# Decay matrices of a gated DeltaNet kept in DRAM, and beta and decay applied per token at R

## The chip, the cores and the metric

The kernel runs on one core of a Trainium2 chip. The core has TensorE (PE, with its weight loads listed as PEld), VectorE (DVE), ScalarE (ACT), GpSimd (POOL) and SyncE (SP), which issues nearly all DMAs. The metric is the device time of one launch in microseconds, the median of several runs.

## The reference

One inference step of a two-layer decoder on 1104 tokens (1024 prompt tokens behind 16 learned ones, and 8 samples of 8 tokens), width 1024. Layer 0 mixes tokens with a gated DeltaNet of 8 heads of 128, layer 1 with a pooling mixer; a gated ConvFFN (2816 wide) follows each. What matters here is the DeltaNet's chunked recurrence:

```python
G = jnp.cumsum(g, axis=-1)
decay = jnp.exp(jnp.where(causal, G[..., :, None] - G[..., None, :], -jnp.inf))
kk = jnp.einsum('bhnid,bhnjd->bhnij', k, k)
lower = jnp.where(strict, beta[..., :, None] * kk * decay, 0.0)
T = lax.linalg.triangular_solve(lower + eye, ...)          # inverse, per chunk
U = jnp.einsum('bhnij,bhnje->bhnie', T, v * beta[..., None])
W = jnp.einsum('bhnij,bhnjd->bhnid', T, k * (beta * jnp.exp(G))[..., None])
A = jnp.einsum('bhnid,bhnjd->bhnij', q, k) * decay
q_dec = q * jnp.exp(G)[..., None]
k_dec = k * jnp.exp(G[..., -1:] - G)[..., None]
def step(S, blk):
    v_new = U_c - W_c @ S
    o = q_dec_c @ S + A_c @ v_new
    S = S * g_tot_c + k_dec_c.T @ v_new
```

So every chunk of every head needs the decay matrix twice: for the triangular inverse and for A. Behind the recurrence o is normalised, gated by z and multiplied by w_out, and the result is added to the residual x.

## The kernel before

Everything is float32. Large products are three TensorE passes on operands that are split into a high and a low part (mm3, L258 to L266); the recurrence's own products are single float32 matmuls of 128 by 128. Tokens stand in nine blocks of 128 (NU): eight of the prompt, and a last one with 16 prompt tokens and the 64 sample tokens ("tail", NTAIL = 80 tokens). GROUPS is three groups of three blocks.

**Stage A (0 to 520 us).** Input projection, causal conv, l2-norm, and for each head k_steps (L479 to L512): it loads the row G of accumulated log decays and the row of beta, broadcast to all partitions (Gb L484, Bb L485), makes E = G_j - G_i plus a mask on DVE (L490, nine instructions), E = exp(E) on ACT (L493), E = E*beta on POOL (L494), stores k (kd, L497), and multiplies k kT by E into Q on DVE (L504). Triangular inverses follow.

**Stage C, the recurrence (520 to about 835 us).** For head h, chain(h) (L1006) walks the eight prompt blocks in order. A block is: pp = (k*exp(G)*beta) S on PE (L1023), R = bv - pp on DVE (L1025), op = q_dec S on PE (L1026), pv = Q R on PE (L1030), vn = pv on ACT (L1032), pS = kd vn on PE (L1036), the new S on DVE (L1041), op += AT vn on PE (L1043). tail(h) (L1058) does the last block. The chain is a string of dependences, so a function weave (L1203) runs fillers between its steps: nxt(h) (L1165), which prepares head h+1, and wouts (L1127), the product with w_out of earlier pairs of heads.

prep(h) (L896) is, for each group: begin() with exp(G) on ACT (L916) and three subtractions on DVE that make E again (L919); scaled() with exp(E) on ACT (L927) and three POOL products, kq[0] = q*exp(G) (L928), eG = exp(G)*beta (L929), kq[1] = k*eG (L930); qk = k q on PE (L937); AT = qk*E on DVE (L939); six transposes of k and v on PE (L944), which ACT scales into kd and bv (L949). begin, scaled and the rest reach their engines through a list (later_on) that the chain empties step by step, so they stand among the chain's instructions on ACT, DVE and POOL in an order fixed when the program is written out.

load(h) (L710) fetches G, beta, q, k and v of a head from DRAM, 576 KB each, each into a tile with one buffer; it is called as soon as the previous head's prep is written out, and each load waits until the last reader of its tile is done. nxt(0) ends with the three loads of the residual x (xT, L1181, 1472 KB each). SP issues DMAs in program order.

gated (L964) normalises o (osq on ACT and DVE, L975 and L986; osb on DVE, L976) as a side job. early_norm (L1122), at the end of stage C, takes the sum of squares of the residual for the first ConvFFN; its tiles come from CT.tile (L1111), out of the five buffers of kq. Behind stage C the ConvFFNs and the pooling mixer run to 2581 us; their weights come through Stream (SP load L161, cast on ACT L153, low part on POOL L154).

Of the kernel before, what the change touches and what calls it, by code (L numbers as in the profile page):

```python
# [10 lines left out]
F32 = mybir.dt.float32  # L11
# [185 lines left out]
def build(nc, tc, I, O, stop=None):  # L197
# [136 lines left out]
    Qd_d = dr.tile([H, P, NTP], F32, name="Qd")  # L334

# [5 lines left out]
    brow_d = dr.tile([H, NTP], F32, name="brow")  # L341

# [136 lines left out]
    def k_steps(h, kT):  # L479
# [14 lines left out]
        G.tensor_tensor(E, E, Bb, op=ALU.mult)  # L494
        Q = kp.tile([P, NU, P], F32, tag="Q", name="Q", bufs=2)
        yield 7
        SY.dma_start(out=kd_d[h], in_=kT)  # L497
        for g0, gn in GROUPS:
            ps = px.tile([P, 3, P], F32, tag="px", name="kk")
            for u in range(gn):  # L500
                s = slice((g0 + u) * P, (g0 + u + 1) * P)
                T.matmul(ps[:, u, :], kT[:, s], kT[:, s], start=True, stop=True)
            q = Q[:, g0:g0 + gn, :]
            V.tensor_tensor(q, ps, v3(E[:, g0 * P:(g0 + gn) * P]), op=ALU.mult)  # L504
            G.affine_select(q, q, pattern=[[0, gn], [1, P]], compare_op=ALU.not_equal, fill=1.0,
                            base=0, channel_multiplier=-1)
            yield 1
# [199 lines left out]
    cl = None  # L707
    Xbd = Tbd = None

    def load(h):  # L710

        t = heads.setdefault(h, {})
        for nm in "GBkqv":
            t[nm] = cl.tile([P, NTP], F32, tag="l" + nm, name="l" + nm)
        SY.dma_start(out=t["G"], in_=grow_d[h:h + 1, :].partition_broadcast(P))
        SY.dma_start(out=t["B"], in_=brow_d[h:h + 1, :].partition_broadcast(P))
        for nm, src in (("q", qd_d), ("k", kd_d), ("v", vd_d)):
            SY.dma_start(out=t[nm], in_=src[h])
# [177 lines left out]
    def prep(h):  # L896
        t = heads[h]
        Gb, Bb = t["G"], t["B"]
# [6 lines left out]
        for gi, (g0, gn) in enumerate(GROUPS):  # L905
# [6 lines left out]
            E = c1.tile([P, 3, P], F32, tag="E", name="E", bufs=2)  # L912
            eG = c1.tile([P, 3, P], F32, tag="eG", name="eG", bufs=2)

            def begin():
                A.activation(eG, v3(Gb[:, s]), AF.Exp)  # L916
                for u in range(gn):
                    m = cm[:, K_MF:K_MF + P] if g0 + u < 8 else cm[:, K_MT:K_MT + P]
                    V.scalar_tensor_tensor(E[:, u, :], Gb[:, (g0 + u) * P:(g0 + u + 1) * P],  # L919
                                           cols[:, g0 + u, 1, h:h + 1], m, op0=ALU.subtract, op1=ALU.add)  # L920
            later_on(begin)
            yield from pause(0.15)
            kq = c2.tile([P, 2, gn, P], F32, tag="kq", name="kq", bufs=5)
            q2 = tl("q2")

            def scaled():
                A.activation(E, E, AF.Exp)  # L927
                G.tensor_tensor(kq[:, 0], v3(t["q"][:, s]), eG, op=ALU.mult)  # L928
                G.tensor_tensor(eG, eG, v3(Bb[:, s]), op=ALU.mult)  # L929
                G.tensor_tensor(kq[:, 1], v3(t["k"][:, s]), eG, op=ALU.mult)  # L930
                A.activation(q2, v3(t["q"][:, s]), AF.Square, scale=P * EPS ** 0.5)
            later_on(scaled)
# [73 lines left out]
    def chain(h):  # L1006
# [5 lines left out]
        for gi, (g0, gn) in enumerate(GROUPS):  # L1012
# [45 lines left out]
    def tail(h, op):  # L1058
# [3 lines left out]
        kq, kd, bv, AT = (t[nm][6] for nm in ("kq", "kd", "bv", "AT"))  # L1062
# [15 lines left out]
        V.tensor_tensor(R[:n], bv[:n, u, :], pp[:n, :P], op=ALU.subtract)  # L1078
# [26 lines left out]
    class CT:  # L1105
# [93 lines left out]
    for h in range(H):  # L1199
# [3 lines left out]
        weave(chain(h), 24.0, [(cur, 7.9 if h else 10.8, 0.0, 0.88, True), (wo, 11.0 if h > 1 else 6.0, 0.0 if h > 1 else 0.45, 1.0, False)], flush_pend)  # L1203
# [481 lines left out]
```

## Time and profile before

| | us |
|---|---|
| median of 3 runs | 2586.09 |
| lowest, highest | 2578.38, 2588.12 |
| the profiled execution's own time | 2583.61 |
| its span in the profile | 2581.5 |
| mean granted TensorE clock | 0.978 |

The profiled execution is the one that all rows below come from. Its span is the time between the first and the last instruction that the profile shows; some 2 us of its own time lie around that. It is 2.5 us below the median of the runs. A stretch is a window from one time in the span to another; in views by window the columns are the busy microseconds and the number of instructions of each engine, the granted clock of TensorE (PEclk, 1.00 is 2.4 GHz and 0.50 is 1.2 GHz), the busy share of the 16 DMA engines, and GB/s.

### The profile page before, as it was taken

What the parts mean: (1) busy time and instruction counts of PE and PEld (TensorE: products, weight loads), DVE (VectorE), ACT (ScalarE), POOL (GpSimd) and SP (SyncE); (2) the same over time, 40 slices, a digit from 0 to 9 for tenths busy, and PEclk for the clock granted to TensorE, in tenths of its full rate; (3) what the DMA queues carried; (4) which work ended last, traced back from release to release, by engine and by line L of the source; (5) the groups of instructions that cost most, each with busy time, mean ns of one, the idle gap of its engine ahead of it and who ended that gap; (6) DMA issues with size and microseconds to landing.
All of it is one profiled execution on the core that took longest, in us unless ns stands there. A gap on an engine that the chain in (4) does not pass through costs nothing.

```text
span 2581.5 us, 38414 instructions
## 1 busy us (share of the span) xinstructions
PE 2415.2 (94%) x14341; PEld 2355.8 (91%) x14341; DVE 1629.9 (63%) x3156; ACT 1029.1 (40%) x2169; POOL 1056.6 (41%) x1103
## 2 busy tenths in 40 slices
PE   6898989979999799999999999888999999999997
PEld 6898988868888799999999999878899999999996
DVE  7566799655666655555555547897964555555556
ACT  5667322354554533322222344445354323223234
POOL 3455322154553443322332465566465333223342
PEclk9999999988999899999999999999999999999999
DMA  3255422476451111111111132233433111111112
GB/s 133 96 183 170 155 78 79 175 251 193 145 176 58 59 53 54 44 39 50 42 50 41 63 111 94 90 110 106 91 100 102 54 46 44 39 50 46 46 54 81
DMA packets 139930, 235.41 MB, mean 91 GB/s; under 512 B 48976, under 2 KB 59600, under 8 KB 139360
## 3 DMA queue, kind: packets, MB, share of 16 engines
q1 hardware_dynamic: 139744, 232.96, 27.3%
q8 instruction: 113, 1.85, 0.3%
q14 instruction: 73, 0.60, 0.1%
HBM read 191.77 MB, written 41.14 MB: 90 GB/s over the span
## 4 chain that ended last, share of the span: by engine, by line
PE 67%; DVE 20%; ACT 5%; issue 3%; POOL 3%; DMA 2%; SPq 0%; DVEq 0%; POOLq 0%; ACTq 0%
PE up L262 12%; PE up L264 12%; PE up L263 12%; PE dn L264 6%; PE dn L262 6%; PE dn L263 6%; DVE acc L385 3%; DVE tb L523 2%; DVE X L525 2%; POOL wlo L154 2%; DVE nhf L317 1%; PE ps L262 1%; PE ps L263 1%; PE ps L264 1%; DVE acc L1262 1%
## 5 line engine op out<-in xcount | busy, mean ns | idle before, releaser
L154 POOL TENSOR_TENSOR wlo<-wst,whi 128x512 fp32r<-128x512 f32 x470 | 631.7, 1362 | 642.3 <-ACT whi L153 629.3
L262 PE MATMUL up<-hhi,whi 128*128 128x370 f32 (+2 forms) x2112 | 709.0, 336 | 0.7 <-ACT hhi L320 0.7
L263 PE MATMUL up<-hlo,whi 128*128 128x370 f32 (+2 forms) x2112 | 700.1, 331 | 2.7 <-DVE hlo L323 1.8
L264 PE MATMUL up<-hhi,wlo 128*128 128x370 f32 (+2 forms) x2112 | 701.5, 332 | 0.0
L1262 DVE SCALAR_TENSOR_TENSOR acc<-up,cv,acc 128x368 f32<-128x368 f32 (+4 forms) x528 | 303.7, 575 | 625.5 <-ACT acc L1254 388.3
L1326 DVE TENSOR_TENSOR xT<-xT,dn 128x368 f32<-128x368 f32 (+1 forms) x864 | 408.9, 527 | 2.4 <-PE dn L264 2.3
L263 PEld LDWEIGHTS up<-hlo,whi 128*128 128x128 f32 x2112 | 402.0, 190 | 5.9 <-DVE hlo L323 2.2
L262 PEld LDWEIGHTS up<-hhi,whi 128*128 128x128 f32 x2112 | 400.4, 190 | 3.0 <-ACT hhi L320 1.0
L264 PEld LDWEIGHTS up<-hhi,wlo 128*128 128x128 f32 x2112 | 400.2, 189 | 0.0
L262 PE MATMUL dn<-ghi,whi 128*128 128x368 f32 (+1 forms) x1056 | 352.9, 334 | 21.7 <-DVE xT L1326 12.4
L264 PE MATMUL dn<-ghi,wlo 128*128 128x368 f32 (+1 forms) x1056 | 349.2, 331 | 0.5 <-POOL wlo L154 0.5
L263 PE MATMUL dn<-glo,whi 128*128 128x368 f32 (+1 forms) x1056 | 348.9, 330 | 0.3 <-POOL glo L1300 0.3
L1254 ACT ACTIVATE acc<-up,cv 128x368 f32<-128x368 f32 (+1 forms) x264 | 173.0, 655 | 431.0 <-PE up L264 429.1
L1300 POOL TENSOR_TENSOR glo<-acc,ghi 128x368 fp32r<-128x368 f32 (+1 forms) x132 | 133.2, 1009 | 485.8 <-ACT ghi L1299 475.9
L262 PE MATMUL ps<-hhi,whi 128*128 128x368 f32 (+1 forms) x792 | 273.5, 345 | 35.2 <-DVE acc L385 29.6
L153 ACT CAST whi<-wst 128x512 fp32r<-128x512 f32 x470 | 274.6, 615 | 78.2 <-PE up L263 50.0
L263 PE MATMUL ps<-hlo,whi 128*128 128x368 f32 (+1 forms) x792 | 269.6, 340 | 5.2 <-DVE hlo L323 3.8
L264 PE MATMUL ps<-hhi,wlo 128*128 128x368 f32 (+1 forms) x792 | 268.3, 339 | 0.0
L262 PEld LDWEIGHTS dn<-ghi,whi 128*128 128x128 f32 x1056 | 200.6, 190 | 26.0 <-DVE xT L1326 7.7
L263 PEld LDWEIGHTS dn<-glo,whi 128*128 128x128 f32 x1056 | 200.7, 190 | 2.0 <-POOL glo L1300 0.6
L264 PEld LDWEIGHTS dn<-ghi,wlo 128*128 128x128 f32 x1056 | 200.5, 190 | 1.0 <-POOL wlo L154 1.0
L262 PEld LDWEIGHTS ps<-hhi,whi 128*128 128x128 f32 x792 | 154.2, 195 | 42.1 <-issue 29.8
(207 smaller groups left out, 3262.8 us busy)
## 6 DMA issues: line engine op xcount, KB each, us to landing
wst<-i_w_up SPq DMA_DIRECT2D x272, 256.0 KB, 2.8
wst<-i_w_dn SPq DMA_DIRECT2D x120, 256.0 KB, 2.7
wst<-i_w_in SPq DMA_DIRECT2D x62, 256.0 KB, 2.8
Gb<-grow SPq DMA_DIRECT2D x8, 576.0 KB, 4.7
Bb<-brow SPq DMA_DIRECT2D x8, 576.0 KB
vd<-out SPq DMA_DIRECT2D x8, 576.0 KB, 2.8
zd<-out SPq DMA_DIRECT2D x8, 576.0 KB, 5.9
kd<-out SPq DMA_DIRECT2D x8, 576.0 KB, 4.1
```

The lines of the kernel that those rows point to most:

```text
L153: self.nc.scalar.copy(hi, st)
L154: self.nc.gpsimd.tensor_tensor(lo, st, hi.bitcast(F32), op=ALU.subtract)
L262: T.matmul(ps, hi[:, ws], rhi(k), start=start and j == 0, stop=False)
L263: T.matmul(ps, hi[:, ws], rlo(k), start=False, stop=False)
L264: T.matmul(ps, lo[:, ws], rhi(k), start=False, stop=stop and j == n - 1)
L385: V.scalar_tensor_tensor(acc[:, a:n], ps[:, o + a - d:o + n - d], w[3 - d], acc[:, a:n], op0=ALU.mult, op1=ALU.add)
L523: V.tensor_tensor(t, X[:n, 0:k, j:j + 1].to_broadcast([n, k, w]), Qb[:n, j:j + 1, j + 1:m].to_broadcast([n, k, w]), op=ALU.mult)
L525: V.tensor_tensor(X[:n, 0:k, j + 1:m], X[:n, 0:k, j + 1:m], t, op=ALU.subtract)
L1254: A.activation(acc[:, b:], ps[:, o + b:o + CH], AF.Identity, scale=w[2], bias=col(C_FCB + l * NUP + n))
L1262: V.scalar_tensor_tensor(acc[:, i:m], ps[:, o + i - d:o + m - d], w[2 - d], acc[:, i:m], op0=ALU.mult, op1=ALU.add)
L1300: G.tensor_tensor(glo, acc, ghi.bitcast(F32), op=ALU.subtract)
L1326: V.tensor_tensor(xT[:, m, s], xT[:, m, s], ps[:, b:CH], op=ALU.add)
```

## The change

In stage A, the exponentiated decay matrix E of each head is stored to DRAM (Ed, 576 KB a head) before k; the POOL product with beta writes to Q instead of E, and DVE multiplies in Q. In stage C, load(h) fetches E instead of beta (five loads as before), and k goes to one of three buffers in rotation instead of one. prep(h) no longer makes E (begin is gone, exp(G) moves into scaled) and has one POOL product a group instead of three; in the last group a POOL and an ACT copy of 128 by 80 fill a tile qk for the tail. In the chain pp = k S is taken from k unscaled, and R = pp*c + bv, where c = -beta*exp(G) stands per token in cols, made once for all heads ahead of the recurrence. early_norm's tiles come from the load tiles of G, q and v instead of kq. The loads of xT move from the end of nxt(0) to right behind load(1). Two cost figures of weave change. The number of TensorE instructions does not.

```diff
@@ k_steps
         A.activation(E, E, AF.Exp)
-        G.tensor_tensor(E, E, Bb, op=ALU.mult)
         Q = kp.tile([P, NU, P], F32, tag="Q", name="Q", bufs=2)
+        G.tensor_tensor(flat(Q), E, Bb, op=ALU.mult)
         yield 7
+        SY.dma_start(out=Ed_d[h], in_=E)
         SY.dma_start(out=kd_d[h], in_=kT)
...
-            V.tensor_tensor(q, ps, v3(E[:, g0 * P:(g0 + gn) * P]), op=ALU.mult)
+            V.tensor_tensor(q, ps, q, op=ALU.mult)
@@ load
-        for nm in "GBkqv":
+        for nm in "GEqv":
             t[nm] = cl.tile([P, NTP], F32, tag="l" + nm, name="l" + nm)
+        t["k"] = (c1 if h % 3 else cl).tile([P, NTP], F32, tag=f"lk{h % 3}", name="lk")
         SY.dma_start(out=t["G"], in_=grow_d[h:h + 1, :].partition_broadcast(P))
-        SY.dma_start(out=t["B"], in_=brow_d[h:h + 1, :].partition_broadcast(P))
-        for nm, src in (("q", qd_d), ("k", kd_d), ("v", vd_d)):
+        for nm, src in (("q", qd_d), ("k", kd_d), ("E", Ed_d), ("v", vd_d)):
             SY.dma_start(out=t[nm], in_=src[h])
@@ prep
-            E = c1.tile([P, 3, P], F32, tag="E", name="E", bufs=2)
+            E = v3(t["E"][:, s])
-            def begin():
+            kq, q2 = tl("kq"), tl("q2")
+            def scaled():
                 A.activation(eG, v3(Gb[:, s]), AF.Exp)
-                for u in range(gn):
-                    m = cm[:, K_MF:K_MF + P] if g0 + u < 8 else cm[:, K_MT:K_MT + P]
-                    V.scalar_tensor_tensor(E[:, u, :], Gb[:, (g0 + u) * P:(g0 + u + 1) * P],
-                                           cols[:, g0 + u, 1, h:h + 1], m, op0=ALU.subtract, op1=ALU.add)
-            later_on(begin)
-            yield from pause(0.15)
-            kq = c2.tile([P, 2, gn, P], F32, tag="kq", name="kq", bufs=5)
-            q2 = tl("q2")
-            def scaled():
-                A.activation(E, E, AF.Exp)
-                G.tensor_tensor(kq[:, 0], v3(t["q"][:, s]), eG, op=ALU.mult)
-                G.tensor_tensor(eG, eG, v3(Bb[:, s]), op=ALU.mult)
-                G.tensor_tensor(kq[:, 1], v3(t["k"][:, s]), eG, op=ALU.mult)
+                G.tensor_tensor(kq, v3(t["q"][:, s]), eG, op=ALU.mult)
                 A.activation(q2, v3(t["q"][:, s]), AF.Square, scale=P * EPS ** 0.5)
+                if gi == 2:
+                    t["qk"] = c2.tile([P, 2, NTAIL], F32, tag="qk", name="qk")
+                    G.tensor_copy(t["qk"][:, 0, :], kq[:, 2, :NTAIL])
+                    A.copy(t["qk"][:, 1, :], t["k"][:, TAIL0:NT])
@@ chain (tail alike)
-                    T.matmul(pp, kq[:, 1, u, :], S, start=True, stop=True)
+                    T.matmul(pp, t["k"][:, c * P:(c + 1) * P], S, start=True, stop=True)
                     R = c2.tile([P, P], F32, tag="R", name="R")
-                    V.tensor_tensor(R, bv[:, u, :], pp, op=ALU.subtract)
+                    V.scalar_tensor_tensor(R, pp, cols[:, c, 1, h:h + 1], bv[:, u, :], op0=ALU.mult, op1=ALU.add)
@@ behind lnexp()
+    A.activation(cols[:, :, 1, :], cols[:, :, 1, :], AF.Exp)
+    V.scalar_tensor_tensor(cols[:, :, 1, :], cols[:, :, 1, :], -1.0, cols[:, :, 0, :], op0=ALU.mult, op1=ALU.mult)
@@ nxt
             load(1)
+            for c in range(NCH):
+                SY.dma_start(out=xT[:, :, ck_(c)], in_=I["xT"][c])
             wd.fetch()
...
             if h == 0:
-                for c in range(NCH):
-                    SY.dma_start(out=xT[:, :, ck_(c)], in_=I["xT"][c])
                 wd.need(1)
```

The order of the instructions shows it at three places. The first is SP's queue during head 0's chain, before: the loads of head 1 (lG, lB, lq, lk, lv), those of w_out and z, the loads of head 2, then xT.

```order
L715 DMA lG<-grow 128x1152
L716 DMA lB<-brow 128x1152
L718 DMA lq<-qd_83 128x1152
L718 DMA lk<-kd_75 128x1152
L718 DMA lv<-vd_91 128x1152
L161 DMA wst<-i_w_out 128x512 x2
L957 DMA lz<-zd_99 128x384 x2
L715 DMA lG<-grow 128x1152
L716 DMA lB<-brow 128x1152
L718 DMA lq<-qd_84 128x1152
L718 DMA lk<-kd_76 128x1152
```

The same place after (the lines are those of the changed kernel).

```order
L720 DMA lG<-grow 128x1152
L722 DMA lq<-qd_83 128x1152
L722 DMA lk<-kd_75 128x1152
L722 DMA lE<-Ed_108 128x1152
L722 DMA lv<-vd_91 128x1152
L1170 DMA xT<-i_xT 128x8x368 x3
L161 DMA wst<-i_w_out 128x512 x2
L954 DMA lz<-zd_99 128x384 x2
L720 DMA lG<-grow 128x1152
L722 DMA lq<-qd_84 128x1152
L722 DMA lk<-kd_76 128x1152
```

xT has moved ahead of the loads of w_out, z and head 2, behind those of head 1; head 2's k stands third in its set instead of fourth.

The second place is DVE's queue in a head in the middle of the recurrence, before: the new S, the subtractions for E, R, two rows of other work, and AT.

```order
L1041 SCALAR_TENSOR_TENSOR S_4844<-S_4843,eGl,pc_4845 128x128
L919 SCALAR_TENSOR_TENSOR E<-lG,cols,cm 128x128 x3
L1025 TENSOR_TENSOR R<-bv,pc_4845 128x128
L1150 TENSOR_TENSOR xT<-xT,wo 128x384
L975 TENSOR_TENSOR osq<-osq,q_6155 128x384
L976 SCALAR_TENSOR_TENSOR osb<-op,cv,lz 128x384
L939 TENSOR_TENSOR AT<-qk,E 128x384
```

The same queue after.

```order
L1038 SCALAR_TENSOR_TENSOR S_4860<-S_4859,eGl,pc_4861 128x128
L1022 SCALAR_TENSOR_TENSOR R<-pc_4861,cols,bv 128x128
L936 TENSOR_TENSOR AT<-qk,lE 128x384
L1148 TENSOR_TENSOR xT<-xT,wo 128x384
L972 TENSOR_TENSOR osq<-osq,q_6080 128x384
L973 SCALAR_TENSOR_TENSOR osb<-op,cv,lz 128x384
```

Nothing stands between the new S and R now, R has another form, and AT stands ahead of the residual's addition and of osq.

The third place is PE's queue where head 0's chain ends and its tail begins, before: the tail's pp, the last block's pv, pS and op, two steps of the tail, and the first qk of head 2.

```order
L1070 MATMUL pp<-kq,Sall 128x2x8 x8
L1030 MATMUL pc_4845<-bv,lQ 128x128
L1036 MATMUL pc_4845<-vn,kd 128x128
L1043 MATMUL op<-AT,vn 128x128
L1075 MATMUL pp<-cm,kqS 80x128
L1076 MATMUL op<-kqS,cm 128x80
L937 MATMUL qk<-lq,lk 128x128 x3
```

The same place after.

```order
L1067 MATMUL pp<-qk,Sall 128x2x8 x8
L1027 MATMUL pc_4861<-bv,lQ 128x128
L934 MATMUL qk<-lq,lk 128x128 x3
L1033 MATMUL pc_4861<-vn,kd 128x128
L1040 MATMUL op<-AT,vn 128x128
L1072 MATMUL pp<-cm,kqS 80x128
L1073 MATMUL op<-kqS,cm 128x80
```

The first qk of head 2 has moved four instructions ahead.

## Rows read from the trace of the kernel before

**Rows 1.** The page: the span, and the busy time of each engine.

```profile
span 2581.5 us, 38414 instructions
PE 2415.2 (94%) x14341; PEld 2355.8 (91%) x14341; DVE 1629.9 (63%) x3156; ACT 1029.1 (40%) x2169; POOL 1056.6 (41%) x1103
```

**Rows 2.** The view by windows, one window a head: from the tail's first pp of one head to that of the next, heads 2 to 6 of the chain. The first number behind the window is its length; then PE, PEld, DVE, ACT and POOL busy with their counts, PEclk, the DMA share and GB/s.

```profile
603.80:642.89 39.09, 36.55 (x261) 34.83 (x261) 25.38 (x61) 19.11 (x57) 17.25 (x16) 0.96 0.48 142
642.89:680.64 37.75, 34.79 (x262) 32.59 (x261) 25.63 (x60) 21.01 (x61) 22.73 (x20) 1.00 0.51 163
680.64:718.25 37.61, 35.06 (x262) 33.35 (x261) 25.18 (x60) 19.12 (x57) 17.08 (x16) 1.00 0.56 171
718.25:755.07 36.82, 34.23 (x263) 32.42 (x261) 24.96 (x60) 20.66 (x60) 21.08 (x19) 1.00 0.50 161
755.07:792.65 37.58, 35.04 (x262) 33.33 (x261) 25.18 (x60) 19.64 (x58) 18.33 (x17) 1.00 0.34 96
```

**Rows 3.** The waits of PE in the same stretch, 603.8 to 792.65 us: who waits, for what, us in total, times, longest.

```profile
PE tr L944 <- DVE AT L939: 5.0, 5, 1.9
PE pc L1030 <- DVE R L1025: 4.2, 4, 1.1
PE tr L944 <- ACT osq L986: 3.5, 5, 0.7
```

**Rows 4.** The timeline of head 4 at one such wait: start, duration, engine, line; in brackets how long the engine had idled and for what.

```profile
694.00 2.97 DVE L919 SCALAR_TENSOR_TENSOR E<-lG,cols,cm 128x128 f32<-128x128 f32 x3
696.89 0.28 DVE L1025 TENSOR_TENSOR R<-bv,pc 128x128 f32<-128x128 f32 x1
697.00 0.52 ACT L927 ACTIVATE E<-E 128x384 f32<-128x384 f32 x1 [2.55 <-DVE E L919]
697.22 0.49 PE L1030 MATMUL pc<-R,lQ 128*128 128x128 f32 x2 [1.03 <-DVE R L1025]
698.42 0.55 PE L944 MATMUL tr<-cm,lv 128*128 128x128 f32 x3 [0.71 <-ACT osq L986]
```

**Rows 5.** The view by windows in head 7's chain, where no prep is left to run.

```profile
780.00:790.00 10.00, 10.00 (x80) 9.99 (x79) 5.34 (x13) 4.16 (x13) 3.98 (x4) 1.00 0.01 2
```

**Rows 6.** All instructions of one line or tile: the subtractions for E, R, and the form of R after the change (the new S at L1041, the same operation with the same kinds of operands but for the side that PSUM is on): least, mean and greatest ns, first and last start.

```profile
L919 DVE SCALAR_TENSOR_TENSOR E<-lG,cols,cm x72: 335/805/2193, 512.7 to 776.6; 128x128 f32<-128x128 f32 x72
L1025 DVE TENSOR_TENSOR R<-bv,pc x56: 271/286/290, 528.4 to 817.0; 128x128 f32<-128x128 f32 x56
L1041 DVE SCALAR_TENSOR_TENSOR Sall<-S,eGl,pc x8: 346/346/351, 553.4 to 819.5; 128x128 f32<-128x128 f32 x8
```

**Rows 7.** The view by windows at the start of the recurrence, heads 0 and 1, and one short stretch of head 2.

```profile
525.00:542.20 17.20, 15.91 (x108) 14.23 (x108) 9.45 (x23) 10.98 (x35) 8.32 (x9) 0.90 0.95 278
542.20:559.80 17.60, 12.79 (x91) 10.70 (x91) 11.21 (x24) 13.49 (x42) 13.06 (x13) 1.00 0.38 124
559.80:565.40 5.60, 0.00 (x1) 0.03 (x1) 4.00 (x4) 0.94 (x2) 5.00 (x5) 0.55 1.00 373
565.40:580.90 15.50, 12.36 (x78) 11.53 (x78) 9.41 (x24) 6.43 (x21) 5.53 (x6) 0.83 1.06 389
580.90:591.00 10.10, 9.37 (x40) 8.32 (x39) 3.78 (x10) 6.15 (x20) 4.84 (x5) 0.50 0.75 180
621.00:626.00 5.00, 4.42 (x21) 4.42 (x21) 2.50 (x7) 3.47 (x13) 1.00 (x1) 0.66 0.00 0
```

**Rows 8.** The timeline of the same stretch, SP's DMA issues (SPq) and the first qk of head 2 on PE.

```profile
532.62 0.32 SPq L715 DMA_DIRECT2D lG<-grow  x1
554.74 0.32 SPq L715 DMA_DIRECT2D lG<-grow  x1
557.91 0.32 SPq L718 DMA_DIRECT2D lk<-kd  x1
559.19 8.04 SPq L1181 DMA_DIRECT2D xT<-i_xT  x3
565.40 1.62 PE L937 MATMUL qk<-lq,lk 128*128 128x128 f32 x6 [5.62 <-DMA lk<-kd]
```

**Rows 9.** The view by windows where the loads of head 1, then those of head 2, then xT keep the DMA engines full, and where nothing is under way.

```profile
538.00:545.00 7.00, 5.75 (x43) 4.88 (x42) 4.99 (x9) 2.17 (x7) 3.36 (x4) 1.00 0.98 383
546.00:555.00 9.00, 6.79 (x46) 5.49 (x46) 5.20 (x15) 8.00 (x26) 5.43 (x6) 1.00 0.00 2
566.00:581.00 15.00, 11.86 (x77) 10.93 (x76) 9.51 (x24) 6.53 (x21) 4.93 (x6) 0.84 1.06 387
```

**Rows 10.** Stage A: DVE's wait for the broadcast rows Gb in 100 to 300 us, in the view of waits (us in total, times, longest).

```profile
DVE E L490 <- DMA Gb<-grow: 35.7, 6, 7.0
```

**Rows 11.** The view by windows in stage A, two stretches between loads and stores.

```profile
216.00:221.00 5.00, 2.75 (x10) 2.62 (x11) 4.35 (x10) 3.28 (x5) 2.54 (x5) 0.80 0.04 15
236.00:240.00 4.00, 3.51 (x20) 3.37 (x21) 3.38 (x9) 3.94 (x6) 2.62 (x6) 1.00 0.03 5
```

**Rows 12.** The page's DMA issues, the store of k in stage A: KB each, median us from issue to landing.

```profile
kd<-out SPq DMA_DIRECT2D x8, 576.0 KB, 4.1
```

**Rows 13.** The timeline at the end of the recurrence: the first loads of the ConvFFN's weights, early_norm's sum of squares on PE, and the first cast of those weights on ACT.

```profile
829.96 30.21 SPq L161 DMA_DIRECT2D wst<-i_w_up  x8
841.48 0.78 PE L295 MATMUL ss<-nac,ck 128*128 128x368 f32 x2
848.50 1.14 ACT L153 CAST whi<-wst 128x512 fp32r<-128x512 f32 x2
```

More of the change, by code (lines that the diff above doesn't have):

```diff
@@ L334, in build @@
     Qd_d = dr.tile([H, P, NTP], F32, name="Qd")
+    Ed_d = [dr.tile([P, NTP], F32, name=f"Ed{h}") for h in range(H)]
     qb_d = dr.tile([P, 64, 64], F32, name="qb")
@@ L706, in build @@
     heads = {}
-    cl = None
+    cl = c1 = None
     Xbd = Tbd = None
@@ L897, in prep @@
         t = heads[h]
-        Gb, Bb = t["G"], t["B"]
+        Gb = t["G"]
         eGl = c2.tile([P, 17], F32, tag="eGl", name="eGl", bufs=3)
@@ L1022, in chain @@
                     pp = pcs[next(npc)]
-                    T.matmul(pp, kq[:, 1, u, :], S, start=True, stop=True)
+                    T.matmul(pp, t["k"][:, c * P:(c + 1) * P], S, start=True, stop=True)
                     R = c2.tile([P, P], F32, tag="R", name="R")
-                    V.tensor_tensor(R, bv[:, u, :], pp, op=ALU.subtract)
-                    T.matmul(op[:, u, :], S, kq[:, 0, u, :], start=True, stop=False)
+                    V.scalar_tensor_tensor(R, pp, cols[:, c, 1, h:h + 1], bv[:, u, :], op0=ALU.mult, op1=ALU.add)
+                    T.matmul(op[:, u, :], S, kq[:, u, :], start=True, stop=False)
                     step()
@@ L1061, in tail @@
         Sall, eGl = t["S"], t["eGl"]
-        kq, kd, bv, AT = (t[nm][6] for nm in ("kq", "kd", "bv", "AT"))
+        kd, bv, AT = (t[nm][6] for nm in ("kd", "bv", "AT"))
         u, n = 2, NTAIL
@@ L1069, in tail @@
             bs = slice(0, N_META) if b == 0 else slice(N_META + (b - 1) * LS, N_META + b * LS)
-            T.matmul(v3(pp[:, :2 * n], n)[:, :, bs], Sall[:, b, :], kq[:, :, 2, bs], start=True, stop=True)
+            T.matmul(v3(pp[:, :2 * n], n)[:, :, bs], Sall[:, b, :], t["qk"][:, :, bs], start=True, stop=True)
         kqS = c2.tile([P, 2 * n], F32, tag="osb", name="kqS")
@@ L1077, in tail @@
         R = c2.tile([P, P], F32, tag="R", name="R")
-        V.tensor_tensor(R[:n], bv[:n, u, :], pp[:n, :P], op=ALU.subtract)
+        V.scalar_tensor_tensor(R[:n], pp[:n, :P], cols[:n, 8, 1, h:h + 1], bv[:n, u, :], op0=ALU.mult, op1=ALU.add)
         yield 1
@@ L1114, in tile @@
             n = self.got.setdefault(tag, [])
-            if len(n) < {"nac": 1, "nsq": 2}[tag]:
-                t = c2.tile([P, 2, 3, P], F32, tag="kq", name=name, bufs=5)
-                n.append(t.rearrange("p a b t -> p (a b t)")[:, :2 * CH].rearrange("p (u t) -> p u t", t=CH))
+            at = {"nac": "G", "nsq": "qv"}[tag]
+            if len(n) < len(at):
+                t = cl.tile([P, NTP], F32, tag="l" + at[len(n)], name=name)
+                n.append(v3(t[:, :2 * CH], CH))
             else:
@@ L1202, in build @@
             early = later.spawn(early_norm())
-        weave(chain(h), 24.0, [(cur, 7.9 if h else 10.8, 0.0, 0.88, True), (wo, 11.0 if h > 1 else 6.0, 0.0 if h > 1 else 0.45, 1.0, False)], flush_pend)
+        weave(chain(h), 24.0, [(cur, 7.45 if h else 10.35, 0.0, 0.88, True), (wo, 11.0 if h > 1 else 6.0, 0.0 if h > 1 else 0.45, 1.0, False)], flush_pend)
     while later.q:
```

## The prediction

> **What bounds the kernel now.** I read four views, in this order. The page first: TensorE is busy 94% of the span, every other engine 63% or less [rows 1], so time is won only where PE idles or runs below its full clock. The change touches nothing behind the recurrence but the hand-over to the ConvFFN, and the number of PE instructions stays, so the question is how much PE idles in stage C and why. The view by windows answers the first half: in heads 2 to 6 PE is busy 36.55, 34.79, 35.06, 34.23 and 35.04 us of 39.09, 37.75, 37.61, 36.82 and 37.58 [rows 2], which leaves 2.54 + 2.96 + 2.55 + 2.59 + 2.54 = 13.18 us idle, some 2.6 a head, nearly the same in each. The view of waits answers the second: 5.0 us for AT, 4.2 for R, 3.5 for osq on ACT, five, four and five times, so about one of each a head [rows 3]. One such place on the timeline shows what they have in common: three subtractions for E hold DVE for 2.97 us, R stands behind them and comes at 696.89, exp(E) on ACT comes at 697.00, and PE, which needs R and then a buffer that ACT frees, waits 1.03 and 0.71 us [rows 4]. All three waits hang on the making of E.
>
> At the start of the recurrence the picture differs. PE idles 17.60 - 12.79 = 4.81 us in the stretch before 559.8 us, then the whole 5.6 us to 565.4, then 15.50 - 12.36 = 3.14 us [rows 7]; the 5.6 us are a wait for the k of head 2, whose load was issued at 557.91 and used at 565.40 [rows 8]. In that idle time the granted clock falls to 0.55; between 580.9 and 591.0 it is 0.50, the lower of the two levels, with PE busy 9.37 of 10.10 us, and between 621 and 626 it is 0.66 [rows 7].
>
> **The steady heads (2 to 6).** Removed: nine subtractions on DVE a head at a mean of 805 ns, 335 to 2193 [rows 6], so 7.2 us of DVE, the exp(E) on ACT, and six of some sixteen POOL products, of about 17.25/16 = 1.1 us each [rows 2]. None of that is on PE; what counts is who stood behind it, and that is R, AT and osq, 12.7 of the 13.18 us idle. Added: R's new form, for which the nearest row is the new S, 346 ns against 286 [rows 6]. Were that 60 ns on the path in each of the 56 R's, it would cost 3.4 us. I take nothing, since two other PE instructions and fillers stand between pp and pv, and in head 7, where there is no prep, the same chain with its fillers keeps PE busy 10.00 of 10.00 us [rows 5]: the chain's own latency is covered there with time to spare. If that cover is gone the price is the 3.4. What is late next is the rest of ACT's and DVE's queues (osq, osb, the additions to xT), which stay. So of 13.18 us I leave half a microsecond a head: 13.18 - 5 x 0.5 = 10.7, taken as **-10.5**; bounds -5 (R and osq only partly freed, the row of AT alone gone) and -13.2.
>
> Which instruction blocks DVE for up to 2193 ns, when its least is 335, can be asked of the Trainium skill. In "SBUF — State Buffer", section "Who interferes with whom", it says that a VectorE instruction with two SBUF inputs contends with a GpSimd instruction that reads SBUF, and that whoever issues first has the port for the whole instruction. The spread of L919 agrees, 335 to 2193 ns beside POOL products of 1.1 us. By that rule the additions for osq, with both inputs in SBUF, can still be held once a head for one POOL product in front of R; the steady term would be -13.18 + 5 x 1.1 = -7.7, and the time 2571.
>
> **The start of the recurrence.** After, the SP queue goes lG, q, k, E, v of head 1, xT, w_out, z, and G, q, k of head 2. The trace shows the DMA engines serve what is issued in turn at 383 to 387 GB/s when full [rows 9]. From about 533 us [rows 8], at that rate: five loads of 0.59 MB to 540.9; xT, 3 x 1.51 = 4.52 MB, 11.7 us, to 552.6; 0.92 MB of w_out and z to 555.0; G, q and k of head 2, 1.77 MB, to 559.6. Before, the set began at 554.74 and its four loads by 387 GB/s would have ended at 560.8; k was used at 565.4, 4.6 us behind that count, part of it since v and xT, issued right behind k, shared the engines. I take about half of the lag over, which puts the landing at 562; with all of it, it is 564.2. The gap of 9 us with nothing under way (546 to 555, 2 GB/s) [rows 9] is what xT fills. PE reaches the first qk of head 2 sooner than at 559.8, since 4.81 us of waits go and four instructions (pS, op and two steps of the tail, some 0.8 us) now stand behind it; so it waits longer than 5.6 us, but until 562. Gain: 565.4 - 562 - 0.8 = **-2.6**, bounds +2.2 (second rival) and -6.6 (k(2) there 4 us sooner). xT is moved past the loads of w_out and z on SP: w_out's first parts land some 2 us behind 554, and ACT's casts of them, with the copies of head 0's last block and of the tail queued behind, are then late by a microsecond or so; PE stands at the qk of head 2 until 562, which covers it. If that wait were not there, this would cost the microsecond.
>
> The Trainium skill, "DMA: Bandwidth & Descriptors", section "Queues, rings and completion order", says that each DMA engine consumes the descriptors of a ring in ring order. The rows agree: k was used 7.5 us behind its issue. By that rule xT in front of head 2 is a price, and without it k(2) would be there at about 558: the sum would be 4 lower, 2564.
>
> Behind 565.4 the 3.14 us idle are of the same kind as in the steady heads; I leave 0.8: **-2.3**, bounds 0 and -3.1. The clock: between 580.9 and 591.0, 9.37 us of work at half the rate cost 4.7; at 621 to 626, 4.42 us at 0.66 about 1.5 to 2.2. Both follow idle PE. The wait for k(2) stays, so a fall of the clock does too; I take half, **-3.5**, bounds 0 and -6.9.
>
> **Stage A.** The store of Ed adds 576 KB a head. There are stretches with the DMA engines nearly idle, shares of 0.04 and 0.03 [rows 11]; the page's store of k takes 4.1 us from issue to landing [rows 12]. DVE waits for Gb in 100 to 300 us 35.7 us in all [rows 10], and where a store is in front of that load it comes 0.59/0.383 = 1.5 us later; in one or two heads of eight the gaps don't cover it. I take **+1**, bounds 0 and +3. The POOL product into Q and DVE's product in place are the same count and size: nothing. c = -beta*exp(G) is two instructions on 72 columns, once.
>
> **The end.** early_norm's tiles now come from the load tiles, and the first weight fetch of the ConvFFN, at 829.96, comes to stand behind instructions near the sum of squares at 841.48. It would land near 845; its first cast runs at 848.50 [rows 13]. Covered by 3.5 us: nothing; if the cover were gone, 2 to 3 us once.
>
> **Sum.** -10.5 - 2.6 - 2.3 - 3.5 + 1 = -17.9. Against the profiled run's own time, 2583.61, that is 2565.7. It ran 2.5 us below the median of 2586.09; from the median the forecast is **2568**, -0.7%.
>
> **Rivals.** (1) The waits change their name. In the steady heads PE waits for R, AT and osq because one of the chain, DVE and ACT is always late, and when E goes another wait of 2.6 us a head takes its place. For: three waits of different engines, all near one a head. Against: head 7, 10.00 of 10.00. Then only the start and the clock gain: -2.6 - 2.3 - 3.5 + 1 = -7.4, 2579.
> (2) xT in front of head 2 costs. At 300 GB/s in place of 385 the same count gives 540.9 + 15.1 + 3.1 + 5.9 + 2 = 567: the start loses 2.2 where it won 2.6, and the clock gain goes: -17.9 + 4.8 + 3.5 = -9.6, 2576. For: k(2) was already 4.6 us later than its own bytes explain. Against: 387 GB/s while xT was loading [rows 9].
> (3) Slower: the store of Ed in front of what stage A waits for. If in each of eight heads the loads of the next stand behind its whole 4.1 us [rows 12], that is 33 us; the sum becomes +14, 2600. It decides from 2.3 us a head (18/8) that the kernel is no faster. For: 35.7 us of waits for Gb already. Against: the gaps [rows 11], and one store at full rate is 1.5 us.
> (4) All goes: the idle of the steady heads, of head 1 and the clock whole: -13.2 - 3.1 - 6.9 - 2.6 = -25.8, 2560.
>
> **How the numbers follow.** Forecast 0.53, (1) 0.20, (2) 0.10, (3) 0.07, (4) 0.10. The likeliest case alone spans 2560 to 2576. The range: down to (4) less the spread of the runs, 2554; up past (1) and (2) with stage A's +3, 2585; (3) is left out, and some of the ends. A measurement of this kernel tells about 0.5% from no change, 12.9 us: faster means under 2573.2. Forecast and (4), 0.63, but for 0.03 that ends above this line: faster 0.60; (1), (2) and that rest: same 0.33; (3): slower 0.07.
>
> **What would show it.** In the windows of the steady heads PE idle of 0.5 us in place of 2.6, no wait for AT, R under 1 us; a timeline where R follows pp without a DVE instruction between; the first qk of head 2 at some 562 us with a wait of 7 us; the clock at 1.00 between 580 and 590 or not; DVE's waits for Gb near 36 us. The forecast is wrong if PE in heads 2 to 6 stays at 2 us idle or more, if k(2) comes later than 565.4, or if stage A ends later than 520 us by more than 3.

## The result, and the profile after

The changed kernel takes 2566.90 us (median of 6 runs, 2566.47 to 2569.03), the kernel before 2581.56 us in the runs beside it (2578.38 to 2588.12). The ratio is 0.994, with a 95% interval of 0.9925 to 0.9955: 0.6% faster, 14.7 us. The forecast was 2568, 0.7% faster, in a range of 2554 to 2585. The forecast's base, 2586.09, was the median of the first three of the six runs of the kernel before. The profiled execution took 2567.12 us.

The page of the changed kernel, its span and its engines:

```profile
span 2565.3 us, 38282 instructions
PE 2411.5 (94%) x14341; PEld 2352.7 (92%) x14341; DVE 1591.5 (62%) x3085; ACT 1021.1 (40%) x2154; POOL 1010.0 (39%) x1063
```

DVE, ACT and POOL have lost 38.4, 8.0 and 46.6 us of work against [rows 1], PE next to none. What PE lost is idle time, and where it lost it the windows tell. The view by windows of the changed kernel, heads 2 to 6, cut at the tail's first pp as in [rows 2] (columns as there):

```profile
596.89:631.96 35.07, 34.51 (x261) 32.99 (x260) 20.76 (x52) 18.06 (x55) 11.32 (x11) 1.00 0.52 159
631.96:668.69 36.73, 34.59 (x262) 32.54 (x261) 20.26 (x51) 20.02 (x59) 16.31 (x15) 1.00 0.53 173
668.69:703.79 35.10, 34.54 (x260) 33.06 (x260) 20.57 (x51) 18.05 (x55) 11.31 (x11) 1.00 0.57 178
703.79:738.77 34.98, 33.80 (x260) 32.19 (x260) 20.26 (x51) 19.57 (x58) 14.92 (x14) 1.00 0.50 163
738.77:773.90 35.13, 34.55 (x260) 33.08 (x260) 20.57 (x51) 18.57 (x56) 12.74 (x13) 1.00 0.40 109
```

The five heads take 773.90 - 596.89 = 177.0 us in place of 792.65 - 603.80 = 188.85, so 11.8 us less. PE idles 0.56 + 2.14 + 0.56 + 1.18 + 0.58 = 5.0 us in place of 13.2, which is 8.2 of the 11.8; another 2.0 are head 2, whose clock was 0.96 with PE busy 36.55 us and is now 1.00 with 34.51. The rest, 0.2 to 0.5 us of busy time in each of the other heads, stays open. The waits of PE in these heads after, which answer to [rows 3]:

```profile
PE tr L941 <- DVE AT L936: 1.5, 2, 0.7
PE ss L981 <- POOL sql L977: 1.4, 5, 0.3
PE tr L941 <- ACT kd L946: 0.9, 4, 0.3
PE pc L1033 <- ACT vn L1029: 0.4, 1, 0.4
PE wo L262 <- DVE xT L1148: 0.3, 1, 0.3
PE pc L1027 <- DVE R L1022: 0.2, 1, 0.2
```

R has gone from 4.2 us to 0.2, osq from 3.5 to nothing, AT from 5.0 to 1.5. What came new (sql, kd) is 0.3 us at a time.

The start, up to the tail of head 1, ends at 596.89 in place of 603.80: 6.9 us less. The wait of 5.6 us for k of head 2 [rows 7, 8] is gone, but another stands in its place. The timeline of the changed kernel, SP's loads, ACT and PE (in brackets the idle time before and what ended it):

```profile
535.72 9.16 SPq L1170 DMA_DIRECT2D xT<-i_xT  x3
544.92 4.85 SPq L161 DMA_DIRECT2D wst<-i_w_out  x2
552.26 0.32 SPq L722 DMA_DIRECT2D lk<-kd  x1
556.86 1.29 ACT L153 CAST whi<-wst 128x512 fp32r<-128x512 f32 x2 [3.83 <-DMA wst<-i_w_out]
558.05 0.26 ACT L1029 COPY vn<-pc 128x128 f32<-128x128 f32 x1
558.37 0.80 PE L1033 MATMUL pc<-vn,kd 128*128 128x128 f32 x2 [4.80 <-ACT vn L1029]
564.03 1.49 PE L934 MATMUL qk<-lq,lk 128*128 128x128 f32 x6
```

The first weights of w_out now lie behind xT in the DMA queue; ACT stands 3.83 us at their cast; vn of head 0's last block stands behind the cast; and PE stands 4.80 us for vn. When PE comes to the first qk of head 2, at 564.03, k is there: no bracket. The clock, by windows:

```profile
553.57:558.37 4.80, 0.00 (x1) 0.01 (x1) 0.00 (x0) 1.46 (x4) 0.82 (x1) 0.79 1.06 392
560.00:571.00 11.00, 10.62 (x65) 10.18 (x64) 3.06 (x10) 4.42 (x16) 4.39 (x4) 0.70 1.10 352
581.00:591.00 10.00, 9.40 (x74) 8.83 (x72) 4.13 (x10) 5.96 (x16) 4.95 (x6) 1.00 0.85 315
```

It still falls after the idle time, to 0.70 over 560 to 571, but the second fall, 0.50 from 580.9 to 591.0 [rows 7], is not there.

Stage A has DVE's wait for Gb as before, 31.8 us in place of 35.7 [rows 10]. The end of the recurrence, which answers to [rows 13], has moved as a whole by 18.5 us: the sum of squares from 841.48 to 822.99, the first cast from 848.50 to 830.01. The cast is 7.0 us behind the sum of squares in both, though the weights' loads are now issued behind that sum. The view of waits (DVE, 100 to 300 us):

```profile
DVE E L492 <- DMA Gb<-grow: 31.8, 6, 6.5
```

And the timeline at the end of the recurrence:

```profile
822.99 0.78 PE L295 MATMUL ss<-nac,ck 128*128 128x368 f32 x2
823.80 17.88 SPq L161 DMA_DIRECT2D wst<-i_w_up  x8
830.01 1.14 ACT L153 CAST whi<-wst 128x512 fp32r<-128x512 f32 x2
```

So the recurrence gave 18.5 us in the two profiled executions, of which the spans keep 2581.5 - 2565.3 = 16.2. The 2.3 us are lost behind it, in code that the change does not touch; at which place stays open.

### The profile page after: what moved, and what is told of

It is laid out like the page before. It is cut to its first block, busy times and chain, and to the rows that moved or that the text cites. A ratio compares the mean times of both kernels' runs of the same rounds, so it can differ in the third digit from the quotient of the medians.

```text
span 2565.3 us, 38282 instructions
## 1 busy us (share of the span) xinstructions
PE 2411.5 (94%) x14341; PEld 2352.7 (92%) x14341; DVE 1591.5 (62%) x3085; ACT 1021.1 (40%) x2154; POOL 1010.0 (39%) x1063
## 4 chain that ended last, share of the span: by engine, by line
PE 65%; DVE 18%; ACT 5%; issue 4%; POOL 3%; DMA 2%; SPq 1%; DVEq 0%; POOLq 0%; ACTq 0%
PE up L264 12%; PE up L262 12%; PE up L263 12%; PE dn L264 6%; PE dn L262 6%; PE dn L263 6%; DVE acc L387 3%; DVE tb L526 2%; POOL wlo L154 2%; DVE X L528 2%; DVE nhf L317 1%; DVE acc L1262 1%; PE ps L262 1%; PE ps L263 1%; PE ps L264 1%
## 5 line engine op out<-in xcount | busy, mean ns | idle before, releaser
L262 PE MATMUL ps<-hhi,whi 128*128 128x368 f32 (+1 forms) x792 | 272.9, 345 | 35.7 <-DVE acc L387 29.9
```

Source lines behind the costliest of these rows:

```text
L262: T.matmul(ps, hi[:, ws], rhi(k), start=start and j == 0, stop=False)
```

## The experiments

Two questions are asked: what in the steady heads carried the gain, the making of E or POOL's products; and what the place of xT's loads is worth. E_made, pool_three, xT_back and wout_first were run as one group, the other four as another. Each ratio is taken to the kernel before, run beside it on the same chip; its medians there were 2582.99 us in the first group and 2584.54 in the second, against 2581.56 beside the change. So runs of different groups are compared here by their ratios, and their medians differ by up to 3 us for the kernel before alone.

| run | median, us | ratio to the kernel before | 95% interval |
|---|---|---|---|
| the change | 2566.90 | 0.9940 | 0.9925 to 0.9955 |
| E_made | 2573.68 | 0.9958 | 0.9944 to 0.9971 |
| pool_three | 2568.31 | 0.9939 | 0.9926 to 0.9951 |
| E_made_pool_three | 2584.47 | 0.9998 | 0.9988 to 1.0008 |
| xT_back | 2570.02 | 0.9944 | 0.9931 to 0.9956 |
| wout_first | 2567.78 | 0.9937 | 0.9925 to 0.9950 |
| xT_late | 2561.27 | 0.9908 | 0.9895 to 0.9921 |
| Ed_store_only | 2585.48 | 1.0001 | 0.9992 to 1.0010 |
| xT_moved_only | 2582.91 | 0.9994 | 0.9983 to 1.0005 |

### E made again

```diff
-        for nm in "GEqv":
+        for nm in "Gqv":
...
-            E = v3(t["E"][:, s])
+            E = c1.tile([P, 3, P], F32, tag="E", name="E", bufs=2)
...
+            def begin():
+                A.activation(eG, v3(Gb[:, s]), AF.Exp)
+                for u in range(gn):
+                    V.scalar_tensor_tensor(E[:, u, :], Gb[...], gcol[:, g0 + u, h:h + 1], m, op0=ALU.subtract, op1=ALU.add)
+            later_on(begin)
...
             def scaled():
-                A.activation(eG, v3(Gb[:, s]), AF.Exp)
+                A.activation(E, E, AF.Exp)
                 G.tensor_tensor(kq, v3(t["q"][:, s]), eG, op=ALU.mult)
```

The diff is cut at the dots; gcol keeps the accumulated log decays per token, which cols no longer holds. With E not loaded, a head has four loads in place of five.

> The changed kernel, but the recurrence makes E again on DVE (nine subtractions a head) and ACT, and does not load it; the stored E is not read. POOL's one product a group, the unscaled k and beta at R stay. Theory (the making of E is what R, AT and osq wait behind): PE idle in heads 2 to 6 goes from 5.0 us back to 11 to 13, time 2574 to 2579. Rival (the POOL products and the new R carried the gain): PE idle stays near 5, time within 2 us of the changed kernel. If POOL's products are what stretches a subtraction to 2.2 us, their mean falls from 805 ns to some 500; if not, it stays at 800.

Measured: 2573.68, just under the low end of the first theory. By the ratios that is 0.0018, some 4.6 us, above the changed kernel, with intervals that overlap; against pool_three, which ran beside it and is equal to the changed kernel by its ratio, it is 5.4 us, and the runs of the two do not overlap (2572.07 to 2574.39 against 2566.95 to 2569.69). In heads 2 to 6, by windows 182.24 us long with PE busy 173.97, PE idles 8.3 us: more than the 5 of the rival, but not the 11 to 13 of the theory. The waits of PE in heads 2 to 6 (600.66 to 782.9 us there):

```profile
PE tr L952 <- DVE AT L947: 5.0, 5, 1.9
PE tr L952 <- ACT osq L994: 1.6, 5, 0.6
PE pc L1038 <- DVE R L1033: 0.8, 1, 0.8
```

The subtractions in the same heads, in the view of groups by line (count, busy us, mean ns, idle time before), in the kernel before (603.8 to 792.65 us) and then in E_made:

```profile
L919 DVE SCALAR_TENSOR_TENSOR E<-lG,cols,cm 128x128 f32<-128x128 f32 x45 | 31.0, 743 | 0.0
```

```profile
L926 DVE SCALAR_TENSOR_TENSOR E<-lG,gcol,cm 128x128 f32<-128x128 f32 x45 | 25.1, 611 | 0.0
```

AT is back at 5.0 as before, but R is at 0.8 and not 4.2, osq at 1.6 and not 3.5, and the subtractions take 611 ns and not 743 on the mean. The 805 ns of [rows 6], which the prediction and the expectation above call a mean, is a median: the view that gives it lists least, median and greatest. Median against median, the fall in heads 2 to 6 is from 807 ns to 344. So the making of E (the subtractions and the exp on ACT, which this run does not tell apart) accounts for the waits for AT, and not by itself for those for R. With one POOL product instead of three in the way the subtractions are shorter, as the second part of the expectation asks, though the mean does not fall to 500.

### Three POOL products again

```diff
                 G.tensor_tensor(kq, v3(t["q"][:, s]), eG, op=ALU.mult)
+                G.tensor_tensor(eG, eG, E, op=ALU.mult)
+                G.tensor_tensor(eG, v3(t["k"][:, s]), eG, op=ALU.mult)
```

> The changed kernel with two more POOL products a group, as many as before, whose results nobody uses. Theory (the making of E carried the gain): PE idle in heads 2 to 6 stays at 5 to 7 us, time 2567 to 2570. Rival (POOL's products hold DVE, or the chain, and their leaving carried it): idle back to 10 or more, time 2574 or more.

Measured: 2568.31, and with a ratio of 0.9939 the same as the changed kernel. PE idles 4.9 us in heads 2 to 6. The first and the third of heads 2 to 6 in its windows are those of the changed kernel but for POOL, which works 17.3 us in place of 11.3:

```profile
597.00:632.16 35.16, 34.59 (x262) 33.07 (x260) 20.88 (x52) 18.05 (x55) 17.32 (x17) 1.00 0.54 161
668.83:703.97 35.14, 34.56 (x260) 33.09 (x260) 20.58 (x51) 18.05 (x55) 17.29 (x17) 1.00 0.57 179
```

POOL's products alone cost nothing that shows. The rival falls in the form that it had; but E_made had left R short, so one more was needed.

### Both together

The two diffs above in one kernel (the second product has q as its operand in place of E).

> E made in the recurrence as in the run E_made, and two more POOL products a group, whose results nobody uses, as in the run pool_three. Theory (the two work together: a POOL product that reads SBUF holds the subtraction that stands behind it on DVE, and R stands behind that): subtractions back from 611 ns to 750 to 800, waits of PE for R back to about 4 us in heads 2 to 6, these heads 186 to 189 us long in place of 182, time 2578 to 2581. Rival (they only add up, and POOL's products cost nothing by themselves, as in pool_three): 182 us, time 2573 to 2575.

Measured: 2584.47, ratio 0.9998: the whole gain is gone (interval 0.9988 to 1.0008), although k stays unscaled, beta enters at R, and xT stands where the change put it. In ratios, making E costs 0.0018, POOL's products nothing, both 0.0058. The subtractions in heads 2 to 6 (602.78 to 796.1 us), in the view of groups by line:

```profile
L926 DVE SCALAR_TENSOR_TENSOR E<-lG,gcol,cm 128x128 f32<-128x128 f32 x45 | 34.5, 820 | 0.0
```

The waits of PE there (603 to 790 us):

```profile
PE tr L954 <- DVE AT L949: 6.5, 5, 1.9
PE pc L1040 <- DVE R L1035: 5.2, 5, 1.1
PE tr L954 <- ACT osq L996: 3.2, 5, 0.6
```

Heads 2 to 4 by windows:

```profile
602.78:642.49 39.71, 36.60 (x261) 34.75 (x260) 26.95 (x61) 19.23 (x58) 17.26 (x17) 0.96 0.36 121
642.49:681.60 39.11, 34.94 (x262) 32.62 (x260) 26.77 (x61) 20.92 (x62) 22.79 (x21) 1.00 0.46 150
681.60:721.58 39.98, 36.60 (x261) 34.76 (x260) 27.12 (x61) 19.23 (x58) 17.25 (x17) 0.96 0.47 138
```

The timeline of one set of subtractions with POOL beside it, and then the subtractions at the same place of E_made:

```profile
615.87 1.01 POOL L933 TENSOR_TENSOR kq<-lq,eG 128x384 f32<-128x384 f32 x1 [1.42 <-ACT eG L923]
616.21 2.97 DVE L926 SCALAR_TENSOR_TENSOR E<-lG,gcol,cm 128x128 f32<-128x128 f32 x3
616.96 1.01 POOL L934 TENSOR_TENSOR eG<-eG,lq 128x384 f32<-128x384 f32 x1
618.04 1.00 POOL L935 TENSOR_TENSOR eG<-lk,eG 128x384 f32<-128x384 f32 x1
```

```profile
614.10 1.34 DVE L926 SCALAR_TENSOR_TENSOR E<-lG,gcol,cm 128x128 f32<-128x128 f32 x3
```

Three subtractions, the shortest of which take 335 ns [rows 6], take 2.97 us beside three POOL products that end at 619.04, and 1.34 us where POOL has one product; in the kernel before it was the same 2.97 us [rows 4]. The wait for R is back at 5.2 us. The heads are longer than expected (193.3 us in all in place of 186 to 189). PE idles 15.8 us in them, 2.6 more than in the kernel before, and two of them run at 0.96 of the clock, with PE busy 36.60 us in place of 34.94.

The Trainium skill, "SBUF — State Buffer", section "Who interferes with whom", says that a VectorE instruction with two SBUF inputs contends with a GpSimd instruction that reads SBUF. The runs agree: a mean of 611 ns with one product a group, 743 (the kernel before) and 820 with three, and no cost of the products where the subtractions are gone.

### xT back in its place

```diff
             load(1)
-            for c in range(NCH):
-                SY.dma_start(out=xT[:, :, ck_(c)], in_=I["xT"][c])
...
             if h == 0:
+                for c in range(NCH):
+                    SY.dma_start(out=xT[:, :, ck_(c)], in_=I["xT"][c])
                 wd.need(1)
```

> The changed kernel with the loads of xT where they were, at the end of head 0's filler. Theory (behind xT the first w_out weights come late, ACT stands at their cast, and vn of head 0 stands behind it): PE's 4.8 us wait for vn goes, a wait of 0 to 3 us for k of head 2 comes, time 2562 to 2565. Rival A (another load of the same stretch ends as late): time within 1 us of 2567. Rival B (xT late delays the loads of head 3 and the first use of xT): slower, 2570 or more.

Measured: 2570.02, in runs from 2565.49 to 2571.46, ratio 0.9944 against 0.9940 of the change: not faster than the changed kernel, and not to be told from it. The theory was half right: the wait for vn went, and the one for k of head 2 did not come; but, as rival A has it, another load of the same stretch is late. PE, on the timeline:

```profile
583.52 1.62 PE L768 MATMUL nw<-Tbd,lQ 128*128 128x128 f32 x6 [3.68 <-DMA Tbd<-xt]
```

The blocks for the inverse of head 2 (Tbd, issued in the tail of head 0) now lie behind xT. The time alone does not decide between rival A (2567) and rival B (2570); the row does.

### w_out first

```diff
             load(1)
+            wd.fetch()
             for c in range(NCH):
                 SY.dma_start(out=xT[:, :, ck_(c)], in_=I["xT"][c])
-            wd.fetch()
```

> The changed kernel with the first two loads of w_out issued ahead of those of xT instead of behind. Theory (as for xT back in its place): PE's 4.8 us wait for vn goes, the k of head 2 lands as before, PE waits 2 us or less for it, time 2563 to 2565. Rival A: PE waits for k of head 2 until 562 or later, time within 1 us of 2567.

Measured: 2567.78, ratio 0.9937, the same as the changed kernel: rival A. The wait for vn went, and that for k of head 2 came back:

```profile
565.34 1.62 PE L934 MATMUL qk<-lq,lk 128*128 128x128 f32 x6 [3.88 <-DMA lk<-kd]
```

So three orders of the same loads give three waits of the same size: 4.8 us for w_out's cast, 3.9 for k, 3.7 for the inverse's blocks. In each of the three, PE waits for something that stands behind xT's 4.5 MB.

### xT later than either

```diff
             load(1)
-            for c in range(NCH):
-                SY.dma_start(out=xT[:, :, ck_(c)], in_=I["xT"][c])
...
         if h + 2 < H:
             load2(h + 2)
+        if h == 0:
+            for c in range(NCH):
+                SY.dma_start(out=xT[:, :, ck_(c)], in_=I["xT"][c])
```

> The changed kernel with the loads of xT behind the loads for the inverse of head 2 (issued in the tail of head 0, near 568 us; the first use of xT is at 591). Theory (the DMA engines are full from 532 to 566 and whatever stands behind xT's 4.5 MB is waited for: w_out's first weights, k of head 2, or the blocks for the inverse of head 2): the waits for vn (4.8), k and the inverse's blocks all go, PE idles under 3 us between 545 and 580, time 2558 to 2562. Rival A (something else is late by as much, such as the first use of xT): within 1.5 us of 2567. Rival B: slower, loads of head 3 behind xT.

Measured: 2561.27, ratio 0.9908 (0.9895 to 0.9921), an interval just below that of the change (0.9925 to 0.9955): the best of all versions here. What it gains on the change is 0.0032, some 8 us, by the ratios, 5.6 us by the medians, and 6.5 us by the spans of the profiled executions (2558.8 and 2565.3). On its timeline SP issues xT at 566.69, behind the blocks for the inverse:

```profile
566.69 4.34 SPq L1086 DMA_DIRECT2D xT<-i_xT  x3
```

The window 545 to 580 of this kernel, and then of the changed kernel:

```profile
545.00:580.00 35.00, 30.60 (x210) 27.72 (x210) 16.19 (x42) 25.32 (x81) 16.27 (x17) 0.90 0.87 286
```

```profile
545.00:580.00 35.00, 26.72 (x176) 23.95 (x175) 14.50 (x38) 20.70 (x67) 13.97 (x14) 0.85 0.89 301
```

PE idles 4.4 us there and not 8.3, above the 3 that was expected, and does 34 more instructions. The waits for w_out's cast, for k of head 2 and for the inverse's blocks are all gone; the one wait for a load that is left between 521 and 605 us is 1.4 us for k of head 1, at 542.3.

### The store of E alone

The kernel before with `SY.dma_start(out=Ed_d[h], in_=E)` in stage A and the POOL product into Q; the stored E is read by nobody.

> The kernel before with only the store of E to DRAM in stage A (and the POOL product into Q that goes with it); nothing reads it. Theory (the store lies in gaps of the DMA engines): 0 to 3 us over the kernel before. Rival (the store stands in front of the loads of Gb): 8 us or more.

Measured: ratio 1.0001 (0.9992 to 1.0010). The store costs nothing that can be measured, to some 2.6 us either way by the interval; DVE's wait for Gb between 100 and 300 us is 33.4 us, 35.7 in [rows 10].

```profile
DVE E L491 <- DMA Gb<-grow: 33.4, 6, 6.5
```

### The move of xT alone

The kernel before with the loads of xT behind load(1).

> The kernel before with only the loads of xT moved behind those of head 1. Theory (what stands behind xT is waited for): the wait of 5.6 us for k of head 2 is replaced by one of 4 to 5 us for vn behind the cast of w_out's first weights; time 0 to 4 us under the kernel before. Rival (the move alone is a loss): 2 us or more over it.

Measured: 2582.91, ratio 0.9994 (0.9983 to 1.0005), 1.6 us under the kernel before and not to be told from it. The wait that I named did not come: ACT idles only 0.23 us at the cast of w_out's weights, since the cast itself is not reached before 562, and k of head 2 is waited for again, 3.9 us in place of 5.6. With the wait for k of head 1, which grew from 1.0 to 2.7 us, it is 6.6 us in all, as in the kernel before. So w_out's weights stand behind xT here too and are hardly waited for: the same move has another neighbour in a kernel whose head 0 is slower. The timeline of ACT:

```profile
562.03 1.29 ACT L153 CAST whi<-wst 128x512 fp32r<-128x512 f32 x2 [0.23 <-DMA wst<-i_w_out]
```

The wait of PE (521 to 605 us; the two are those for k of head 1 and of head 2):

```profile
PE qk L937 <- DMA lk<-kd: 6.6, 2, 3.9
```

## Why the prediction was right, and where it was not

**The time.** 2568 against 2566.90 is in part luck. The base of the forecast, 2586.09, lies 4.5 us above the median of all six runs, 2581.56; of the 17.9 us that the sum takes off, 14.7 came by the medians and 16.5 between the profiled executions (2583.61 and 2567.12). Two things that the sum does not have partly cancel: 1.6 us less busy time in heads 3 to 6, and 2.3 us lost behind the recurrence.

**The steady heads, forecast -10.5.** PE's idle time fell by 8.2 us, inside the bounds of -5 and -13.2; the term was 2.3 too large, since 5.0 us of small waits stayed and not 2.5 (head 3 alone idles 2.14, over the 2 us that the prediction names as a sign of being wrong, the five heads 1.0 on the mean). That the waits sat in DVE's and ACT's queues behind the making of E was right, but only in part: E_made shows that with E made again R waits 0.8 us, and E_made_pool_three that it takes the three POOL products as well to bring back 5.2. The change took away both of two things that together cost 15 us (0.9998 - 0.9940 = 0.0058 of 2584); taking away the two POOL products alone gives some 10 of it (0.9998 - 0.9958), taking away the making of E alone all 15 (0.9998 - 0.9939), each to some 4 us by the intervals.

The prediction had the two together as a sentence on the rule that it takes from the Trainium skill, not in the sum. The -7.7 that it gives by that rule lies near the measured -8.2, but not for its reason: osq's additions are not held, 550 ns at 128x384 in the changed kernel and 568 in the kernel before, and R hardly waits. What grew is osb's product (L987 at 128x336, a mean of 1171 ns in place of 589 at L990 before), and PE does not wait for it. Nine subtractions a head at their mean of 743 ns are 6.7 us of DVE and not 7.2; the sum does not use that figure.

**R's new form, forecast nothing.** Shown: R takes some 60 ns more, and in heads 2 to 6 PE waits for it 0.2 us, once.

**The wait for k of head 2, forecast -2.6.** The step that failed is the cover: "PE stands at the qk of head 2 until 562, which covers it". The section on the change calls the pv, pS and op ahead of that qk head 0's last block, and the prediction goes by that; they are the first block of head 1. The vn that stands behind w_out's cast is that of head 0's last block, ahead of the tail's pp on PE, so the cast holds PE before it ever comes to the qk, and the wait for k cannot cover it. PE waits 4.80 us there, and k is in time. The DMA count itself was about right: w_out's weights were forecast some 2 us behind 554 and were cast at 556.86. The 7.5 us from the issue of k to its use, which the prediction names for the order of the loads, are a time and not an order; what bears the order out is that k of head 2 is not waited for where it stands ahead of xT (xT_back), and is waited for 3.9 us behind it (wout_first). That the place of xT had a price was right: 5.6 to 8 us, the difference to xT_late; and that an xT in its old place would be better (the 2564 of the prediction) was wrong: xT_back is not faster, for the inverse's blocks. In rival (2) the same count gives a loss of 2.4 us at the start and not 2.2, which changes nothing.

**The clock and head 1, forecast -3.5 and -2.3.** With the term above -8.4 in all. Up to the tail of head 1 the profiled executions differ by 6.9, and head 2's recovered clock adds 2.0: 8.9. The view by windows from 520 us to that point, before and after:

```profile
520.00:603.80 83.80, 64.68 (x419) 58.49 (x417) 45.55 (x98) 47.54 (x142) 45.05 (x42) 0.86 0.81 267
```

```profile
520.00:596.89 76.89, 61.90 (x415) 56.46 (x414) 29.41 (x75) 44.79 (x137) 27.82 (x27) 0.89 0.88 290
```

Idle time fell by 4.1 us, where k and head 1 were to give 4.9, and busy time by 2.8, which with head 2's 2.0 makes 4.8 where the clock was to give 3.5. The sum came out, but with a wait in it that the prediction did not have, so that it is near is luck as well. Of the two falls of the clock named, both went (581 to 591 and 621 to 626), while the one behind the first long wait stayed, at 0.70 over 560 to 571.

**Stage A, forecast +1; the end, nothing.** The store costs nothing that shows (1.0001). The first R of the recurrence starts at 529.9 us in place of 528.4 [rows 6]; how much of that is stage A's was not separated. The late fetch at the end is covered: the first cast keeps its 7.0 us behind the sum of squares.

**The rivals.** Waits that change their name: no, 5.0 against 13.2 us. xT in front of head 2: a price, but smaller than the gain; the start is 6.9 us shorter and not longer. The store of E in front of Gb: no. That all goes (2560): the change alone does not reach it, the change with xT late does, at 2561.

## What to carry to other kernels

When an engine's instruction takes a multiple of its least time beside another engine's, ask about the pair: here taking away either one would have given most of the gain, and a test of one part alone misleads. A large load that nobody needs yet can be paid for by whoever stands behind it in the DMA queue: list the first users of all that follows, and put it behind the last of them that is near. A wait covers a delay only if it stands ahead of the delayed instruction's user, so read which block and which head a row belongs to before naming the cover.

## What was not expected of the hardware

A short idle time can cost twice. In E_made_pool_three, heads of nearly the same number of TensorE instructions (261 to 263) differ by the clock: 0.96 with PE busy 36.60 us, 1.00 with 34.94; the kernel before has one such head in its profile [rows 2, 7], the changed kernel none. In the first of these heads of E_made_pool_three the clock is at its lower level for some 3.5 us, right behind as long a stretch in which PE idles half the time:

```profile
618.00:621.50 3.50, 1.76 (x12) 1.33 (x11) 3.37 (x7) 2.28 (x8) 1.00 (x1) 1.00 0.02 5
621.50:625.00 3.50, 3.50 (x16) 3.50 (x15) 1.26 (x4) 2.46 (x8) 1.03 (x2) 0.51 0.00 0
```

What decides between a fall and none is not shown: in E_made PE is busy 6.61 of the 10 us from 652 to 662, and the clock stays at 1.00. The runs of the two kernels with such heads in their profiles also scatter more: 2579.52 to 2588.77 for E_made_pool_three and 2578.38 to 2588.12 for the kernel before, against 2566.47 to 2569.03 for the change, 2572.07 to 2574.39 for E_made and 2560.57 to 2562.79 with xT late (11 and 6 runs against 6, 5 and 4). That such falls of the clock, 1.7 us each, are what scatters is argued from these windows; it was not shown run by run.
